# A fixed TensorE order, paired inversions and a spilled matrix in the scan of a hybrid RWKV-7 layer

## The chip, the cores and the metric

The kernel runs on one core of a Trainium2 chip. A core has five engines that run side by side: TensorE (matmuls, written PE in the profile, with its weight loads as PEld), VectorE (DVE), ScalarE (ACT), GpSimd (POOL) and SyncE (SP), which here only issues transfers. Each engine, and each queue of transfers, works through its instructions strictly in the order that was fixed when the program was compiled; semaphores make it wait for others. The metric is the device time of one execution in microseconds, as the median of several runs. Times of single instructions come from one profiled execution.

## What is computed

One layer of a latent generator: a modulated RMSNorm, one input projection (2048 to 6400 columns), a bidirectional RWKV-7 time mixing over 16 heads of 64, a pooling branch, and one output projection with a gated residual. There are 1024 latent tokens and 256 context tokens, whose final scan state is where the latent scans begin. Cut to what matters:

```python
def reference(x, c, ctx, ...):
    ...
    p_l = h_l @ w_in[l]
    p_c = h_c @ w_in[l]
    lat = rwkv_prepare(centred_token_shift(p_l[..., :N_SHIFT], shift_mu[l]), ...)
    cx = rwkv_prepare(centred_token_shift(p_c[..., :N_SHIFT], shift_mu[l]), ...)
    S0 = jnp.zeros((N_DIR, B, N_HEADS, HEAD_DIM, HEAD_DIM), jnp.float32)
    S_ctx, y_c = bidir_scan(S0, *cx)
    _, y_l = bidir_scan(S_ctx, *lat)
    ...
    out_l = branch_output(p_l, y_l, r_l, kd_l, v_l, ...)
    x = x + gt_l * out_l
    return rms_norm(x, final_g)

def _rwkv_step(S, inp):
    r, w, k, v, a, b = inp
    sa = jnp.einsum('dbhvk,dbhk->dbhv', S, a)
    S = S * w[..., None, :] + sa[..., :, None] * b[..., None, :] + v[..., :, None] * k[..., None, :]
    y = jnp.einsum('dbhvk,dbhk->dbhv', S, r)
    return S, y
```

## The kernel before

Three stages follow each other on the time axis.

**Preparation** (lines 185 to 546). Dense matmuls in three f16 products (`dense_mm`, lines 152 to 154) make the columns of r, k and v for the pairs of heads j = 0 to 7; `prep_scan` (line 422) turns them into the scan's operands and stores these in DRAM: `sAR` (A and R rows), `sBK` (B and K rows), `sV` and `sBV`. The work on pair j runs beside the dense matmuls of pair j + 1. Pair 7 has no successor: after its last dense tile only its own chain is left (the tail). Its last TensorE work is the bonus product (lines 497 and 498), in the PSUM banks B1 and A1.

**Scan** (lines 555 to 948). Time is cut into 20 chunks of 64 tokens, 4 context and 16 latent. Four quarters Q, each of four heads in both directions, go through 20 chunks, so there are 80 steps, in 20 batches of four. What a step needs:

- `scores` (line 650): 16 small f32 matmuls (as the profile counts them, two to a product) of the B/K rows with the A/R rows into the banks A0 and A1; VectorE masks them into NA and, for latent chunks, MR. Four diagonal blocks of NA go to a DRAM tile `dn`.
- `inverse` (line 688), once per batch: the 32 x 32 diagonal blocks of four steps are gathered from `dn` into TT, 64 on the partitions, and inverted on VectorE by 30 pairs of instructions (tm on line 702, TT on line 704). The result goes through DRAM into T, and TensorE joins the blocks with 64 + 64 tiny matmuls (lines 726 and 737).
- `step` (line 769): X = NA times SUV (line 787), a VectorE copy Xs, T times Xs (line 800), two VectorE copies into SUV, then the state product (line 811), the VectorE sum St, two VectorE products into the next step's SUV (line 818) and a GpSimd product S (line 819). The outputs of a latent step (lines 827 and 829, 32 matmuls) are emitted late, after X of the step behind it.
- `load_step` (line 743), one step ahead: v rows, A rows, B/K rows with four transposes (line 761), R.
- `finish` (line 854): normalisation and gating of two finished chunk pairs.

What is left of the dense input projection (24 tiles of 96 matmuls: gate and pooling columns) is the `filler`, a generator that is advanced one unit (12 dense matmuls) at a time by `pump`. One GpSimd queue (`idma`) and one SyncE queue (`dma`) carry the transfers.

The order on every engine, TensorE too, is made by the planner of the tile framework: it takes what is ready, by priority. A priority is the place in the program text, moved forward by the offset of a `high_priority` block: 800 for the four phases of a step, 1000 for the scores, inversions and finishes beside it, none for the filler. The first two batches are prepared ahead of the steps, with FILL0 = 10 units of filler in the text. Buffers: NA and MR ten each, TT two.

**Output projection** (lines 952 to 1044). 2 x 4 x 16 blocks of three fp32r products (line 981), residual and final norm.

Of the kernel before, what the change touches and what calls it, by code (L numbers as in the profile page):

```python
# [31 lines left out]
RING = 10  # L32
BVS = 2
WRAW = 2
FILL0 = 10
SCT = (1, 3, 5, 7)
INVT = 10
HP_STEP = 800
HP_SIDE = 1000
# [19 lines left out]
def hybrid_layer_kernel(ctx: ExitStack, tc: tile.TileContext, I, out, dbg=None):  # L59
# [22 lines left out]
    sV = dram.tile([4, NCH, 2, C, 2, C], F32, name="sV")  # L82
    sG = dram.tile([8, 128, NTOK], F32, name="sG")
# [471 lines left out]
    with ExitStack() as p2s:  # L555
# [31 lines left out]
        def pool_tile(jj, z):  # L587
            g = jj // 2
            win = WINDOWS[g]
            for x in lat_tile(34 + jj):  # L590
                if x is None:
                    yield
                    continue
                i, ps = x
                S.activation(up[:, :, 8:72], ps.rearrange("p (r t) -> p r t", t=C), AF.Copy, scale=1.0 / HW)
                a = p2.tile([128, 8, 80], F32, tag="pa", name=nm("pa"))
                V.tensor_tensor(a[:, :, 1:80], up[:, :, 0:79], up[:, :, 1:80], ALU.add)
                lo, hi, half = 1, 79, 1
                while 2 * half < win:
                    b = p2.tile([128, 8, 80], F32, tag="pb" if half != 2 else "pa", name=nm("pb"))  # L600
                    lo, hi = lo + half, hi - half
                    V.tensor_tensor(b[:, :, lo:hi + 1], a[:, :, lo - half:hi + 1 - half], a[:, :, lo + half:hi + 1 + half], ALU.add)
                    a, half = b, 2 * half
                zv = z[:, 512 * i:512 * i + 512].rearrange("p (r t) -> p r t", t=C)
                V.tensor_tensor(zv, a[:, :, 8:72], rc[:, g].unsqueeze(1).broadcast_to([128, 8, C]), ALU.mult)
                V.tensor_tensor(zv, zv, up[:, :, 8:72], ALU.subtract)
                yield

        def pool_group(g):
# [3 lines left out]
            for m in range(2):  # L613
                wpool = p2.tile([128, 2, 128], F32, tag="wpool", name=nm("wpool"))
                dma(wpool, I["w_pool"][:, g, :, 128 * m:128 * m + 128])
                for x in lat_tile(42 + 2 * g + m):
# [4 lines left out]
                    sg = silu_gate(ps)  # L621
                    for k in range(2):
# [16 lines left out]
        NFILL = 24 * 10  # L639

        st8 = {}

        hss = [slice(64 * h, 64 * h + 64) for h in range(2)]

        def get(Q, g):
            if (Q, g) not in st8:
                st8[(Q, g)] = dict(SUV=[], NA=[], MR=[], BKt=[])
            return st8[(Q, g)]

        def scores(Q, g, s):  # L650
            b = get(Q, g)
# [5 lines left out]
            dma(AR.rearrange("q a p d t -> q (a p d t)"), sAR[Q, c, :, 0:ns].rearrange("q a p d t -> q (a p d t)"))  # L657
            NA = p2.tile([128, 2, 2, 2, C], F32, tag="NA", bufs=RING, name=nm("NA"))
            MR = None
            if g:  # L660
                MR = p2.tile([128, 2, 2, 2, C], F32, tag="MR", bufs=RING, name=nm("MR"))
            b["NA"].append(NA)
            b["MR"].append(MR)
            ps = [bank(f"A{h}") for h in range(2)]
            for p in range(2):
                for d in range(2):
                    u = 2 * p + d
                    for h in range(2):
                        hs = hss[h]
                        mm(ps[h][:, 64 * ns * u:64 * ns * (u + 1)], BK[hs, p, d, :], AR[hs, :, p, d, :], start=True, stop=True)  # L670
            for h in range(2):
                pv = ps[h][:, 0:256 * ns].rearrange("q (p d a t) -> q p d a t", p=2, d=2, a=ns)
                V.tensor_tensor(NA[:, h], pv[:, :, :, 0, :],
                                mask[:, h, :, 0:64].unsqueeze(1).broadcast_to([128, 2, 2, C]), ALU.mult)
            if s == 0:
                b["dn"] = dram.tile([2, 2, 4, 4, 32, 32], F32, tag="dn", bufs=3, name=nm("dn"))
            for blk in range(2):
                for h in range(2):
                    rs = 64 * h + 32 * blk
                    dma(b["dn"][blk, h, s].rearrange("u s t -> s u t"),  # L680
                        NA[rs:rs + 32, h, :, :, 32 * blk:32 * blk + 32].rearrange("q p d t -> q (p d) t"))
            for h in range(2):
                if g:
                    pv = ps[h].rearrange("q (p d a t) -> q p d a t", p=2, d=2, a=2)
                    V.tensor_tensor(MR[:, h], pv[:, :, :, 1, :],
                                    mask[:, h, :, 64:128].unsqueeze(1).broadcast_to([128, 2, 2, C]), ALU.mult)

        def inverse(Q, g):
            b = get(Q, g)
            c0 = CCH * g  # L690
            NA = b["NA"]
            TTf = p2.tile([128, 32, 32], F32, tag="TT", bufs=2, name=nm("TT"))
            TT = TTf[0:64]
            idma(TT.rearrange("q a b -> q (a b)"), b["dn"].rearrange("k h c u s t -> (k h c u) (s t)"))
# [4 lines left out]
            for s in range(30, 0, -1):  # L699
                n = 31 - s  # L700
                tm = p2.tile([64, s, n], F32, tag="tm", name=nm("tm"))
                V.tensor_tensor(tm, TT[:, 0:s, s:s + 1].broadcast_to([64, s, n]),  # L702
                                TT[:, s:s + 1, s + 1:32].broadcast_to([64, s, n]), ALU.mult)
                V.tensor_tensor(TT[:, 0:s, s + 1:32], TT[:, 0:s, s + 1:32], tm, ALU.add)  # L704
                if s % 3 == 0:
                    yield
            V.memset(TT.rearrange("q a b -> q (a b)")[:, 0:1024:33], 1.0)
            T1c = TTf[64:96]
            V.tensor_copy(T1c, TT[0:32].rearrange("q a b -> q b a"))
            dt = dram.tile([2, 2, 16, 32, 32], F32, tag="dt", bufs=2, name=nm("dt"))  # L710
            dtt = dram.tile([2, 16, 32, 32], F32, tag="dtt", bufs=2, name=nm("dtt"))
            idma(dtt.rearrange("h u s t -> (h u) (s t)"), T1c.rearrange("q a b -> q (a b)"))
            idma(dt.rearrange("k h u s t -> (k h u) (s t)"), TT.rearrange("q a b -> q (a b)"))
            T1 = p2.tile([128, 16, 32], F32, tag="T1", name=nm("T1"))
            for h in range(2):
                idma(T1[64 * h:64 * h + 32], dtt[h].rearrange("u s t -> s u t"))
            for h in range(2):
                for blk in range(2):
                    rs = 64 * h + 32 * blk
                    idma(T[rs:rs + 32, :, 32 * blk:32 * blk + 32], dt[blk, h].rearrange("u s t -> s u t"))  # L720
# [22 lines left out]
        def load_step(Q, g, s):  # L743
            b = get(Q, g)
            SUV = p2.tile([128, 2, 2, 2, C], F32, tag="SUV", bufs=SVB, name=nm("SUV"))
            c = CCH * g + s
            for h in range(2):
# [3 lines left out]
            b["SUV"].append(SUV)  # L751
            for h in range(2):
                dma(b["NA"][s][hss[h], h].rearrange("q p d t -> q (p d) t"),
                    sAR[Q, c, hss[h], 0].rearrange("q p d t -> q (p d) t"))
            if c < NCH - 1:
                BK = p2.tile([128, 2, 2, 128], F32, tag="BK", bufs=BKB, name=nm("BK"))
                dma(BK.rearrange("q p d x -> q (p d x)"), sBK[Q, c].rearrange("q p d s t -> q (p d s t)"))
                BKt = p2.tile([128, 2, 2, 2, C], F32, tag="BKt", bufs=BTB, name=nm("BKt"))
                pst = bank(f"B{c % 2}")
                for u in range(4):  # L760
                    nc.tensor.transpose(pst[:, 128 * u:128 * u + 128], BK[:, u // 2, u % 2, :], ident)  # L761
                S.copy(BKt.rearrange("q p d h t -> q (p d h t)"), pst)
                b["BKt"].append(BKt)
            if g:
# [358 lines left out]
```

## Time and profile before

| | us |
|---|---|
| three runs, median (lowest to highest) | 2388.03 (2385.95 to 2404.02) |
| the profiled execution | 2389.13 |
| its span, first to last instruction | 2387.4 |
| last dense tile of pair 7 ends, first filler matmul | 897.0 |
| first scores matmul | 965.2 |
| first X | 1042.6 |
| last X | 1979.4 |
| last filler matmul | 2018.7 |

The mean granted clock was 0.988 of full speed. In a row of the stretches "busy" is the time in which at least one instruction of the engine was under way; matmuls are pipelined, so one starts before the one ahead has ended. A row of a group gives line, engine, operation, what is written and read, the shape and count, then busy us and mean ns, then the idle time ahead of it and what ended it. A row of the timeline gives start and length in us, and in square brackets the idle time ahead of it.

### The profile page before, as it was taken

How to read it: one execution, taken by the hardware profiler on the slowest of the kernel's cores; microseconds unless marked ns; L12 is line 12 of the kernel's file. 1: busy time of each engine (PE TensorE's matmuls, PEld its weight loads, DVE VectorE, ACT ScalarE, POOL GpSimd, SP SyncE). 2: the span in 40 equal slices, each digit the busy share in tenths (PEclk: the TensorE clock that was granted, in tenths of full speed). 3: DMA queues.
4: the chain of work that ended last, by engine and by line, in shares of the span. 5: the costliest groups of instructions: out<-in, count | busy, mean ns of one | idle time of the engine just before them, and what ended most of it. 6: DMA issues, size and time to landing. Idle time of an engine off the chain costs nothing. (4 is left out here: it accounts for less than half of the span.)

```text
span 2387.4 us, 50718 instructions
## 1 busy us (share of the span) xinstructions
PE 2252.8 (94%) x19854; PEld 1342.6 (56%) x19854; DVE 1637.4 (69%) x3432; ACT 785.7 (33%) x1307; POOL 380.2 (16%) x682
## 2 busy tenths in 40 slices
PE   2999999999999999899999999999999999999997
PEld 1445444454454454446655566556665655888886
DVE  7644756566466567588698888999888884345446
ACT  5334533444444434112122212312231222333424
POOL 3000000000000001023333333333333321000000
PEclk9999999999999999999899999999999999999999
DMA  8665556455354355655556556555666432645546
GB/s 309 218 215 159 152 144 157 134 147 147 96 129 113 87 138 144 175 152 145 159 147 169 151 141 181 165 148 158 179 171 167 134 95 92 234 133 169 190 128 207
DMA packets 421598, 374.60 MB, mean 157 GB/s; under 512 B 232984, under 2 KB 298552, under 8 KB 421104
## 3 DMA queue, kind: packets, MB, share of 16 engines
q1 hardware_dynamic: 403824, 331.75, 48.1%
q0 software_dynamic: 17536, 39.61, 5.8%
q8 instruction: 157, 2.57, 0.4%
q14 instruction: 81, 0.66, 0.1%
HBM read 286.53 MB, written 83.37 MB: 155 GB/s over the span
## 5 line engine op out<-in xcount | busy, mean ns | idle before, releaser
L152 PE MATMUL ps<-hhi,whi 128*128 128x512 f16 x1600 | 611.5, 383 | 2.6 <-ACT whi L144 2.0
L154 PE MATMUL ps<-hhi,wlo 128*128 128x512 f16 x1600 | 611.3, 383 | 1.4 <-DVE wlo L145 1.3
L153 PE MATMUL ps<-hlo,whi 128*128 128x512 f16 x1600 | 610.4, 382 | 0.4 <-DVE hlo L247 0.4
L152 PEld LDWEIGHTS <-whi 128*128 128x128 f16 x1888 | 185.2, 98 | 182.0 <-issue 27.6
L154 PEld LDWEIGHTS <-wlo 128*128 128x128 f16 x1888 | 185.0, 98 | 177.4 <-issue 18.1
L153 PEld LDWEIGHTS <-whi 128*128 128x128 f16 x1888 | 185.4, 98 | 165.7 <-issue 14.8
L144 ACT ACTIVATE whi<-wraw 128x512 f16<-128x512 f32 x200 | 123.1, 628 | 262.4 <-PE ps L153 196.3
L702 DVE TENSOR_TENSOR tm<-TT 64x30 f32<-64x30 f32 (+2 forms) x600 | 195.8, 326 | 16.8 <-DMA TT<-dn 7.9
L704 DVE TENSOR_TENSOR TT<-TT,tm 64x30 f32<-64x30 f32 (+2 forms) x600 | 196.5, 328 | 8.5
L981 PE MATMUL ps<-wolo,mhi 128*128 128x512 f32 x512 | 199.7, 390 | 2.2 <-DVE wolo L977 2.1
L977 DVE TENSOR_TENSOR wolo<-wo,wohi 128x512 fp32r<-128x512 f32 x144 | 97.9, 690 | 148.1 <-ACT wohi L976 147.9
L145 DVE SCALAR_TENSOR_TENSOR wlo<-wraw,whi 128x512 f16<-128x512 f32 x200 | 135.9, 684 | 92.2 <-ACT whi L144 90.8
L981 PE MATMUL ps<-wohi,mlo 128*128 128x512 f32 x512 | 198.9, 389 | 0.0
L981 PE MATMUL ps<-wohi,mhi 128*128 128x512 f32 x512 | 198.2, 390 | 0.4 <-ACT wohi L976 0.4
L976 ACT CAST wohi<-wo 128x512 fp32r<-128x512 f32 x144 | 89.1, 621 | 177.3 <-PE ps L981 150.1
L670 PE MATMUL ps<-AR,BK 64*128 64x128 f32 (+1 forms) x1280 | 121.7, 294 | 16.3 <-DMA BK<-sBK 7.3
L670 PEld LDWEIGHTS ps<-AR,BK 64*128 64x128 f32 x1280 | 104.5, 196 | 44.7 <-issue 14.6
L750 POOL DMA_DIRECT2D SUV<-sV x160 | 96.6, 607 | 124.9 <-PE ps L811 62.4
L981 PEld LDWEIGHTS ps<-wolo,mhi 128*128 128x128 f32 x512 | 96.1, 188 | 24.1 <-DVE wolo L977 4.2
L981 PEld LDWEIGHTS ps<-wohi,mhi 128*128 128x128 f32 x512 | 95.9, 188 | 21.6 <-ACT wohi L976 2.0
L981 PEld LDWEIGHTS ps<-wohi,mlo 128*128 128x128 f32 x512 | 96.1, 188 | 19.7
L819 POOL TENSOR_TENSOR S<-St,PCt 128x256 f32<-128x256 f32 x76 | 56.9, 749 | 258.1 <-DVE St L813 228.6
(226 smaller groups left out, 3379.3 us busy)
## 6 DMA issues: line engine op xcount, KB each, us to landing
wraw<-in_w_in SPq DMA_DIRECT2D x200, 256.0 KB, 3.4
BK<-sBK SPq DMA_DIRECT2D x156, 256.0 KB, 3.5
wo<-in_w_out SPq DMA_DIRECT2D x144, 256.0 KB, 3.0
wa<-in_w_ada SPq DMA_DIRECT2D x112, 256.0 KB, 3.1
wg<-in_w_ada SPq DMA_DIRECT2D x64, 256.0 KB, 3.1
AR<-sAR SPq DMA_DIRECT2D x64, 256.0 KB, 3.0
sBK<-BK SPq DMA_DIRECT2D x32, 320.0 KB, 3.9
sBK<-BK SPq DMA_DIRECT2D x16, 640.0 KB, 5.5
```

The lines of the kernel that those rows point to most:

```text
L144: S.activation(whi, raw, AF.Copy, scale=WS)
L145: V.scalar_tensor_tensor(wlo, raw, WS, whi, op0=ALU.mult, op1=ALU.subtract)
L152: mm(ps[:, :n], w[0][:, k, :], hi[kt][:, o:o + n], start=(kt == 0), stop=False)
L153: mm(ps[:, :n], w[0][:, k, :], lo[kt][:, o:o + n], start=False, stop=False)
L154: mm(ps[:, :n], w[1][:, k, :], hi[kt][:, o:o + n], start=False, stop=(kt == KT - 1))
L670: mm(ps[h][:, 64 * ns * u:64 * ns * (u + 1)], BK[hs, p, d, :], AR[hs, :, p, d, :], start=True, stop=True)
L702: V.tensor_tensor(tm, TT[:, 0:s, s:s + 1].broadcast_to([64, s, n]), TT[:, s:s + 1, s + 1:32].broadcast_to([64, s, n]), ALU.mult)
L704: V.tensor_tensor(TT[:, 0:s, s + 1:32], TT[:, 0:s, s + 1:32], tm, ALU.add)
L750: (idma if d else dma)(SUV[hss[1 - h], h, :, d, :], sV[Q, cn, h])
L976: S.copy(whi, raw)
L977: V.tensor_tensor(wlo, raw, whi.bitcast(F32), ALU.subtract)
L981: mm(banks[q, t], mix[k][m][:, tk], w, start=(k == order[0] and n == 0), stop=(k == order[-1] and n == 2))
```

## The change

TensorE's order in the scan is no longer planned. The whole scan stands in a block in which TensorE keeps the order of the text; the other engines are still planned, with new offsets (steps 800, side work 600, inversions 100). The text is written out step by step in `run_step`: X, the outputs of the step before, T, scores of the step 15 ahead (LEAD), state product, transposes of the next step, then filler in three portions, 2.15 units a step while there are scores and 3.2 in the last 15. Ahead of the steps stand 15 times one unit and one `scores`, then the first assembly with four units.

Two batches are inverted at once: `inverse(i)` works on 128 partitions for the batches 2i and 2i + 1, in the second to sixth of eight steps, and the joining of the blocks moves into `assemble`, once per batch (in the seventh and eighth step for the first batch of the pair, in the following first and second for the other). NA has 15 buffers. MR has two; it is stored to a DRAM tile `sMR` after its scores and loaded again one step before its outputs. Loads are split off: `score_loads` one step ahead of the scores, `step_loads` and the A rows (`a_rows`) one step ahead of X. The sums of the pooling branch go in two halves, and the pool product has a unit of its own.

```diff
-RING = 10
+RING = 15
...
-FILL0 = 10
-SCT = (1, 3, 5, 7)
-INVT = 10
+LEAD = 15
+FILLS = (2.15, 3.2)
 HP_STEP = 800
-HP_SIDE = 1000
+HP_SIDE = 600
+HP_INV = 100
...
+    sMR = dram.tile([4, NCH - CCH, 128, 512], F32, name="sMR")
...
+                for q in range(2):
+                    r4 = slice(4 * q, 4 * q + 4)
+                    a = p2.tile([128, 4, 80], F32, tag="pa", name=nm("pa"))
+                    V.tensor_tensor(a[:, :, 1:80], up[:, r4, 0:79], up[:, r4, 1:80], ALU.add)
...
                     sg = silu_gate(ps)
+                    yield
...
+            if g:
+                MR = p2.tile([128, 2, 2, 2, C], F32, tag="MR", bufs=2, name=nm("MR"))
+                for h in range(2):
+                    V.tensor_tensor(MR[:, h], pv[h][:, :, :, 1, :],
                                     mask[:, h, :, 64:128].unsqueeze(1).broadcast_to([128, 2, 2, C]), ALU.mult)
-
-        def inverse(Q, g):
+                dma(sMR[Q, c - CCH], MR.rearrange("q h p d t -> q (h p d t)"))
+
+        def inverse(i):
+            TT = p2.tile([128, 32, 32], F32, tag="TT", name=nm("TT"))
+            idma(TT.rearrange("q a b -> q (a b)"), dns[i].rearrange("k e h c u s t -> (k e h c u) (s t)"))
+            for s in range(30, 0, -1):
+                n = 31 - s
+                tm = p2.tile([128, s, n], F32, tag="tm", name=nm("tm"))
...
+        def run_step(k):
+            r = k % 8
+            part = FILLS[k + LEAD >= NST] / 3
+            inv = invs.get(k // 8 + 1)
+            last = k == NST - 1
+            with chain():
+                phase_x(k)
+            with side():
+                if not last:
+                    step_loads(k + 1)
+                    if (k + 1) % 4:
+                        a_rows(k + 1)
+                if k + LEAD + 1 < NST:
+                    score_loads(k + LEAD + 1)
+                if r in (0, 6) and k // 4 + 1 + (r == 6) * 0 < len(batches):
+                    asm["now"] = assemble(k // 4 + 1)
+                    next(asm["now"])
+                if st.get("late"):
+                    outputs()
+                elif k:
+                    suv.pop(k - 1)
+            if not (k and steps[k - 1][1]):
+                pump(1)
+                owed[0] -= 1
+            with chain():
+                phase_t(k)
+            with side():
+                if r in (1, 7) and "now" in asm:
+                    run(asm.pop("now"))
+                    if r == 7 and not last:
+                        a_rows(k + 1)
+                if k + LEAD < NST:
+                    scores(k + LEAD)
+                else:
+                    fin_tick()
+            with chain():
+                phase_s(k)
+            with side():
+                if r == 3 and not last:
+                    a_rows(k + 1)
+                if not last:
+                    turned(k + 1)
+            pump(part)
+            with tc.high_priority(offset=HP_INV):
+                if r == 0 and k // 8 + 1 < NST // 8:
+                    invs[k // 8 + 1] = inverse(k // 8 + 1)
+                elif inv is not None and 1 <= r <= 5:
+                    for _ in range(2 + (r == 5)):
+                        next(inv, None)
+            pump(part)
+            with side():
+                if r in (0, 6) and "now" in asm:
+                    next(asm["now"])
+                fin_tick()
+            pump(part)
+            with side():
+                fin_tick()
+
+        with tc.manual_schedule(engines={mybir.EngineType.PE}):
+            for k in range(LEAD):
+                with side():
+                    score_loads(k)
+                pump(1)
+                with side():
+                    scores(k)
+                    if k == 7:
+                        invs[0] = inverse(0)
+                    elif k > 7:
+                        next(invs[0], None)
+                        next(invs[0], None)
+            with side():
+                score_loads(LEAD)
+                run(invs[0])
+                step_loads(0)
+                asm["now"] = assemble(0)
+                next(asm["now"])
+            pump(1)
+            with side():
+                turned(0)
+            pump(1)
+            with side():
+                next(asm["now"])
+            pump(1)
+            with side():
+                run(asm.pop("now"))
+                a_rows(0)
+            pump(1)
+            for k in range(NST):
+                run_step(k)
+            with side():
+                if st.get("late"):
+                    outputs()
+            run(fill)
+            for f in fins:
+                run(f)
```

More of the change, by code (lines that the diff above doesn't have):

```diff
@@ L750, in load_step @@
                     (idma if d else dma)(SUV[hss[1 - h], h, :, d, :], sV[Q, cn, h])
-            b["SUV"].append(SUV)
-            for h in range(2):
[L753 to L763, printed above, removed]
@@ new lines, in turned, with phase_x @@
+        def turned(k):
+            if k not in ins:
+                return
+            BK = ins.pop(k)
+            BKt = bkts[k] = p2.tile([128, 2, 2, 2, C], F32, tag="BKt", bufs=BTB, name=nm("BKt"))
+            pst = bank(f"B{k % 2}")
+            for u in range(4):
+                nc.tensor.transpose(pst[:, 128 * u:128 * u + 128], BK[:, u // 2, u % 2, :], ident)
+            S.copy(BKt.rearrange("q p d h t -> q (p d h t)"), pst)
+        st = {}
+        def phase_x(k):
+            Q, g, s = steps[k]
+            NA, SUV = get(Q, g)["NA"].pop(s), suv[k]
+            if g + s == 0:
+                S0 = st["S"] = p2.tile([128, 4, C], F32, tag="S", bufs=2, name=nm("S"))
@@ L790, in step @@
[L790 to L800 removed]
+            XU = st["XU"] = bank("XU")
+            for u in range(4):
+                for h in range(2):
+                    mm(XU[hss[h], 64 * u:64 * u + 64], NA[:, h, u // 2, u % 2, :], SUV[:, h, u // 2, u % 2, :],
+                       start=True, stop=True)
@@ L801, in step, with phase_t @@
+            Xs = st["Xs"] = p2.tile([128, 4, C], F32, tag="Xs", name=nm("Xs"))
+            V.tensor_copy(Xs.rearrange("q u v -> q (u v)"), XU[:, 0:256])
+        def phase_t(k):
+            Q, g, s = steps[k]
+            T, XU, Xs, SUV = get(Q, g)["T"], st["XU"], st["Xs"], suv[k]
+            for u in range(4):
+                for h in range(2):
+                    mm(XU[hss[h], 256 + 64 * u:320 + 64 * u], T[hss[h], 4 * s + u, :], Xs[hss[h], u, :], start=True, stop=True)
             for h in range(2):
@@ L847, in step, with outputs @@
-            if g:
-                if last:
-                    outputs()
-                else:
-                    carry["late"] = outputs
-            yield
+                st["S"] = Sn
+            st["late"] = (k, DY, S0) if g else None
+        def outputs():
+            k, DY, S0 = st["late"]
+            Q, g, s = steps[k]
+            SUV, MR, R = suv.pop(k), mrs.pop(k), rts.pop(k)
+            ous = [(u, h, DY[hss[h], 256 + 64 * u:320 + 64 * u]) for u in range(4) for h in range(2)]
+            for u, h, o in ous:
+                mm(o, MR[:, h, u // 2, u % 2, :], SUV[:, h, u // 2, u % 2, :], start=(u == 0), stop=False)
+            for u, h, o in ous:
+                mm(o, R[hss[h], u // 2, u % 2, :], S0[hss[h], u, :], start=False, stop=(u == 3))
+            i = CCH * g + s - CCH
+            if i == 0:
+                st["y"] = {}
+            ys = st["y"]
+            if i < 8 and i % 2 == 0:
+                m = (6 - i) // 2
+                ys[m] = p2.tile([128, 2, 2, 2, C], F32, tag=f"y{m}", name=nm("y"))
+            yv = DY[:, 256:512].rearrange("q (p d v) -> q p d v", p=2, d=2)
+            for d in range(2):
+                cn = 15 - i if d else i
+                m = (7 - cn) // 2 if cn < 8 else (cn - 8) // 2
+                y = ys[m][:, :, cn // 8, cn % 2, :]
+                if i < 8:
+                    S.copy(y, yv[:, :, d, :])
+                else:
+                    V.tensor_tensor(y, yv[:, :, d, :], y, ALU.add)
+            if i > 8 and i % 2:
+                fins.append(finish(Q, (i - 9) // 2, ys[(i - 9) // 2]))
```

262 lines of the change are left out of this document (95 added, 167 removed).

## The prediction

> **What bounds the kernel now.** I read the page first, then the busy time by stretch, then the timeline around one step, then the counts by line. The columns of the stretches are: length, busy us (x instructions) of PE, PEld, DVE, ACT, POOL, then granted clock, DMA share, GB/s.
>
> ```profile
> span 2387.4 us, 50718 instructions
> PE 2252.8 (94%) x19854; PEld 1342.6 (56%) x19854; DVE 1637.4 (69%) x3432; ACT 785.7 (33%) x1307; POOL 380.2 (16%) x682
> ```
> ```profile
> 897.00:956.00 59.00, 57.62 (x267) 26.00 (x266) 44.68 (x55) 25.87 (x36) 9.91 (x20) 1.00 0.57 151
> 956.00:1042.00 86.00, 76.80 (x492) 39.60 (x491) 56.47 (x152) 11.24 (x19) 9.52 (x15) 0.94 0.58 164
> 1042.00:1979.00 937.00, 906.09 (x11836) 565.52 (x11834) 798.20 (x2209) 217.62 (x401) 316.00 (x496) 0.99 0.55 153
> 1979.00:2021.00 42.00, 41.67 (x283) 20.33 (x283) 13.65 (x27) 8.64 (x15) 3.13 (x5) 1.00 0.24 79
> ```
>
> TensorE is the bound everywhere the change reaches. The stretches are: the tail of the preparation (to 956), scores and first inverse (to 1042), the 80 steps (to 1979), filler left over (to 2021). In the last three TensorE idles 9.2 + 30.9 + 0.3 = 40 us, and the clock (0.94 of 86 us, 0.99 of 937 us) costs 5 + 9 = 14 us more: some 55 us are there to be won as waits. VectorE is the second engine, 798 of 937 us.
>
> Busy time hides a second loss, which the timeline of one step shows in its start times.
>
> ```profile
> 1503.38 0.38 PE L154 MATMUL ps<-hhi,wlo 128*128 128x512 f16 x1
> ...
> 1503.69 0.68 PE L800 MATMUL ps<-Xs,T 64*64 64x64 f32 x16
> ...
> 1504.30 0.39 PE L152 MATMUL ps<-hhi,whi 128*128 128x512 f16 x1
> ...
> 1505.17 0.38 PE L153 MATMUL ps<-hlo,whi 128*128 128x512 f16 x1
> ...
> 1505.48 0.33 PE L811 MATMUL ps<-SUV,BKt 128*64 128x64 f32 x2
> ...
> 1505.74 0.39 PE L154 MATMUL ps<-hhi,wlo 128*128 128x512 f16 x1
> ...
> 1505.97 0.38 PE L152 MATMUL ps<-hhi,whi 128*128 128x512 f16 x1
> ...
> 1506.28 0.68 PE L811 MATMUL ps<-SUV,BKt 128*64 128x64 f32 x14
> ...
> 1506.89 0.39 PE L153 MATMUL ps<-hlo,whi 128*128 128x512 f16 x1
> ...
> 1509.07 0.68 PE L787 MATMUL ps<-SUV,NA 128*64 128x64 f32 x14 [0.16 <-DVE SUV L818]
> ...
> 1509.68 0.56 PE L829 MATMUL ps<-S,R 64*64 64x64 f32 x12
> ```
>
> A dense matmul lasts 0.38 us but, dense after dense, the next starts 0.216 us later; before a small f32 one it takes 0.31 (1503.38 to 1503.69, 1505.17 to 1505.48), so going into small work costs 0.09. Small matmuls start about 0.04 apart, and the last of a block needs some 0.15 to the next dense one (14 of L811 take 0.61: 13 x 0.035 + 0.15), so going back costs 0.11. One excursion is 0.2 us, all of it "busy". A change between two kinds of small work costs about 0.1 (14 of L787 take 0.61 to L829). TensorE leaves the dense stream 418 times between 950 and 2025 in the timeline, one step's S product even in two pieces as above: 418 x 0.2 = 84 us, and about 350 changes among the small kinds, 35 us.
>
> The Trainium skill, "Trainium Kernel Development and Optimization", section Performance Expectations, calls matmul busy time a bad metric of how near a kernel is to its bound, because matmuls are pipelined. The trace agrees (0.38 long, 0.216 apart). By busy time alone the order of the instructions could win nothing beyond the idle 40 us, and the sum below would be 2452 in place of 2404.
>
> **The change part by part.**
>
> *1. The cover of the preparation's tail goes: +49 us.* Columns as above, of one line alone; then rows of TensorE, SyncE's queue and ScalarE.
>
> ```profile
> 897.00:956.00 59.00, 30.59 (x81) 7.85 (x81) 1.00 0.57 151
> ...
> 897.00:956.00 59.00, 30.20 (x81) 7.93 (x81) 1.00 0.57 151
> ...
> 897.00:956.00 59.00, 29.96 (x79) 7.77 (x80) 1.00 0.57 151
> ```
> ```profile
> 951.15 0.81 PE L497 MATMUL ps<-kdh,headr 128*128 128x512 f32 x2
> ...
> 965.23 1.11 PE L670 MATMUL ps<-AR,BK 64*128 64x64 f32 x16 [1.77 <-DMA AR<-sAR]
> ```
> ```profile
> 954.20 0.33 SPq L500 DMA_DIRECT2D sBV<-bv  x1
> ...
> 956.97 0.86 SPq L766 DMA_DIRECT2D R<-sAR  x2
> ...
> 959.94 0.42 SPq L656 DMA_DIRECT2D BK<-sBK  x1
> ```
>
> From 897 the last head pair's preparation is a chain of VectorE and DMA work. TensorE stays busy only because the scheduler pulls 81 + 81 + 79 = 241 dense filler matmuls (20 units of 12) ahead of the first scores. In the new text the order on TensorE is one unit, scores(0), one unit, scores(1). scores(0) takes bank A1, which the last bonus product (L497 at 951, i = 1) holds, and its loads stand on SyncE's queue behind the last store of the preparation (954.20). So scores(0) comes at about 957 at best (issue plus some 3 us), and only one unit, 12 matmuls, can stand before it. The other 229 are paid later: 229 x 0.216 = 49 us. The tail itself I take as no shorter: its chain runs through VectorE and stores, not through the filler.
>
> *2. Fewer changes of kind: -48 us.* In the new text a step is X, outputs, T, scores, S, turn, then about 2.15 units in one piece. Dense blocks: 80 (steps) + 17 (the unit after X where there are no outputs) + 14 and 8 (third unit behind an assemble or a finish) + 19 (lead) + 32 (pool products) = 170, at 0.2 = 34 us. Changes among small kinds: some 0.45 us a step, 36 us. Before 84 + 35 = 119, after 70. The work itself (dense, scores, X, T, S, outputs, turns, assembles) is the same number of instructions.
>
> *3. Two batches in one inversion: VectorE -206 us, on the path nothing by itself.*
>
> ```profile
> L704 DVE TENSOR_TENSOR TT<-TT,tm 64x30 f32<-64x30 f32 (+2 forms) x600 | 196.5, 328 | 8.5
> L702 DVE TENSOR_TENSOR tm<-TT 64x30 f32<-64x30 f32 (+2 forms) x600 | 195.8, 326 | 16.8 <-DMA TT<-dn 7.9
> ...
> L802 DVE COPY SUV<-ps 64x256 f32<-64x256 f32 x160 | 67.1, 419 | 22.5 <-PE ps L800 19.2 <-issue 0.4
> ...
> L789 DVE COPY Xs<-ps 128x256 f32<-128x256 f32 x80 | 32.8, 410 | 7.1 <-PE ps L787 6.2 <-PE ps L827 0.9
> ```
>
> A copy on 128 partitions takes what one on 64 takes (410 against 419 ns), so 1200 instructions become 600 at the same 0.33: -196 us, and ten transposed copies of 1.03 fewer, -10. VectorE falls from 798 to about 600 of some 940 us. The halved pool sums add a few us there, hidden. VectorE is not the bound, so this pays only through shorter waits (part 5). The price is the delay of the first inversion (part 5).
>
> *4. MR through DRAM, loads a step ahead: 0.* Per step one store and one load of 256 KB more; on SyncE's queue two issues of about 0.4 (rows like the BK load above), 8 to 9 us of a step of 11.7 (937 / 80). The DMA engines stand at 0.55. MR's load waits for the outputs of the step before and holds behind it on SyncE the A rows and the score loads of the next step; they have a step in hand. If that cover went, each late load would stop TensorE, 0 to 1 us a step; nearest row 0.86 for two issues. I take 0.
>
> *5. Waits: 55 before, 69 after: +14 us.*
>
> ```profile
> 1511.71 1.05 DVE L709 COPY TT<-TT 32x1024 f32<-32x1024 f32 x1
> ...
> 1512.91 0.40 DVE L789 COPY Xs<-ps 128x256 f32<-128x256 f32 x1
> ...
> 1513.37 0.54 PEld L800 LDWEIGHTS ps<-Xs,T 64*64 64x64 f32 x16 [0.60 <-DVE Xs L789]
> ```
> ```profile
> 1027.26 1.08 POOL L713 DMA_DIRECT2D dt<-TT  x1 [10.87 <-DVE tm L702]
> ...
> 1032.29 1.29 POOL L716 DMA_DIRECT2D T<-dtt  x2
> ```
> ```profile
> L726 PE MATMUL ps<-T,NA x1280: 184/191/254, 1037.7 to 1946.4; 32*32 32x32 f32 x183
> ```
>
> X was done at 1509.75 (L787 above), its copy ran at 1512.91: VectorE's queue delays a hand-off by 3 us today and TensorE fills the time with whatever is ready. With a fixed order the cover is what the text puts there. X to T: copy 0.41 and about 0.2 of signalling against 32 output matmuls, 1.24 us; T to S: two copies, 0.84 + 0.2, against 16 score matmuls, 1.3 us. The cover is enough unless VectorE is inside another instruction (0.3 to 1.05 us). I take 0.2 a step over 65 steps, 13 us; bounds 0 and 1.0. In the last 15 steps there are no scores behind T: 1.1 each, 16 us. First inversion: it needs eight steps' scores and shares VectorE with seven more; from its last instruction to L726 the trace has 10.4 us (1027.3 to 1037.7), while TensorE's lead text holds about 72 us of work: a wait of 15 us, bounds 0 and 30. Nine later assembles, 1 us each, bounds 0 and 5. The last finish is no longer covered by dense work after 1979: 6 us. Clock: 10. Sum 69.
>
> *Sum:* 49 - 48 + 14 = +15. The profiled execution took 2389.1 us (span 2387.4 and 1.7 around it), 1.1 above the median 2388.0 of the three runs. 2389.1 + 15 = 2404 us.
>
> **The rivals.**
>
> *A, faster: the scores start inside the tail.* If the planner puts scores(0) and the next ones ahead of the bonus product, the 15 units of the lead, 180 matmuls, fill the tail and part 1 falls to about zero: 2404 - 49 = 2355. For it: the loads now carry a priority. Against it: bank A1, and the first instruction of the scan's pool runs at 948 today, behind the last head pair's sum:
>
> ```profile
> 948.36 0.31 POOL L777 MEMSET S<- 128x256 f32 x1 [1.36 <-DVE kds L487]
> ```
>
> *B, slower: the hand-offs decide.* Each step has two places (T and S) where TensorE now stands still if VectorE is late. The wait of 3.2 us above, of which the cover takes 1.2, is what such a place can cost. With 0.8 us a step in place of 0.2, 80 x 0.6 = 48: 2452. From 0.3 us a step on (0.2 + 8/80) the result is over 1% slower. For it: VectorE carries in five of eight steps all inversions, about 3.9 us on top of 6. Against it: it has 200 us less to do.
>
> *C, slower: each inversion ends late and stops TensorE.* The two-batch inversion ends in the sixth of eight steps, its assemble stands at the end of the seventh, 10 us later, about what store and load take. If it is 4 us late each time, 9 x 4 = 36: 2440.
>
> ```profile
> 965.00:990.00 25.00, 23.95 (x149) 12.83 (x150) 8.04 (x16) 1.82 (x3) 0.54 (x1) 0.86 0.47 132
> ...
> 1165.00:1190.00 25.00, 24.87 (x307) 16.79 (x308) 15.80 (x46) 3.65 (x9) 6.00 (x10) 0.88 0.46 128
> ```
> The granted clock has dips of 0.86 and 0.88 over 25 us, 3 us each; the first follows the idle 1.77 before L670 at 965, so gaps of 4 us could cost 3 more each: 9 x 3 = 27, 2467 with C. The Trainium skill, "TensorE: Matmul & The Clock Gate", in the table under "Why this matters for your kernels", warns of idle gaps over about 3 us, after which the clock halves; the dips agree in kind, though gaps of under 3 us stand before them here.
>
> **How the numbers follow.** Forecast (waits as summed, part 1 in full): 0.42, own range 2380 to 2425. A 0.22. B 0.24. C 0.12. About 1%, 24 us, is what a measurement of this kernel can tell from no change, so under 2364 is faster and over 2412 slower. The forecast holds the middle, A the faster side, B and C the slower: 0.22, 0.42, 0.36. The range for 8 in 10 reaches from just under A's 2355 to B's 2452, 2350 to 2452.
>
> **What would show it.** Part 1: dense filler matmuls before 956 fall from 241 to about 12, and TensorE is idle for some 45 us before the first scores. If it is busy there, A holds. Part 2: a timeline with dense runs of 12 to 36 and some 170 excursions. Part 3: tm and TT rows x300 each at 0.33. Part 5: TensorE's idle in the steps, by what ended it: Xs and SUV copies (B), T loads or the assemble (C). I am wrong if the idle time in the tail stays small, or if the steps hold under 15 or over 100 us of waits.

## The result and the profile after

| | before | after |
|---|---|---|
| median, us (lowest to highest) | 2394.07 (2385.95 to 2404.02) | 2422.64 (2419.09 to 2425.25) |
| the profiled execution, us (span) | 2389.13 (2387.4) | 2419.09 (2417.3) |
| first filler matmul, first scores, first X | 897.0, 965.2, 1042.6 | 894.0, 954.1, 1046.2 |
| dense filler matmuls ahead of the first scores | 274 | 12 |
| last X, last filler matmul | 1979.4, 2018.7 | 2029.4, 2042.6 |

The changed kernel takes 1.0116 times as long, 95% interval 1.0068 to 1.0165: 28 us or 1.2% slower, in four runs of each. The prediction had 2404 us; its sum was +15 us on the profiled execution, which became +30.

The page of the kernel after, then its four stretches (columns as in the prediction: length, busy us and instructions of PE, PEld, DVE, ACT, POOL, granted clock, DMA share, GB/s):

```profile
span 2417.3 us, 50344 instructions
PE 2169.6 (90%) x19854; PEld 1312.0 (54%) x19854; DVE 1495.2 (62%) x2868; ACT 794.4 (33%) x1311; POOL 356.4 (15%) x652
```
```profile
894.00:954.00 60.00, 11.84 (x38) 4.27 (x36) 37.67 (x43) 19.00 (x24) 5.89 (x15) 0.57 0.45 111
954.00:1046.00 92.00, 75.65 (x588) 40.54 (x588) 44.47 (x124) 7.96 (x14) 16.04 (x25) 0.85 0.73 211
1046.00:2029.00 983.00, 892.78 (x12070) 565.89 (x12072) 681.21 (x1692) 241.56 (x429) 290.66 (x464) 0.97 0.61 178
2029.00:2050.00 21.00, 17.03 (x181) 9.28 (x180) 9.13 (x19) 6.01 (x11) 2.58 (x4) 1.00 0.39 127
sum 1156.00, PE 997.30 PEld 619.97 DVE 772.48 ACT 274.52 POOL 315.17; mean PE 249.32 PEld 154.99 DVE 193.12 ACT 68.63 POOL 78.79
```

These rows hold the whole account. Before, the same work filled 1124 us (897 to 2021) with 1082 us of busy TensorE; now it fills 1156 with 997. TensorE issues the same 19854 matmuls and is busy 85 us less, which is what the order was to bring and more. But it stands idle for 159 us in place of 42: 117 us of new waits. Together that is 32 us more; the stretch begins 3 us earlier than before and 1 us more follows it, so 30 remain. What TensorE waited for from 890 to 2060 (waiting instruction, what ended the wait, us in total, times, longest):

```profile
PE ps L826 <- DVE Xs L819: 38.4, 26, 3.8
PE ps L498 <- ACT kdh L492: 37.4, 1, 37.4
PE ps L628 <- DVE sg L576: 21.5, 10, 3.7
PE ps L839 <- DVE SUV L828: 20.2, 20, 4.5
PE ps L153 <- ACT whi L145: 10.4, 1, 10.4
PE ps L839 <- DVE y L875: 8.0, 6, 2.6
PE ps L682 <- DMA AR<-sAR: 7.0, 2, 5.8
```

Second row: the preparation's tail, where the bonus product (L498) now waits in the open. L826 is T times Xs and L839 the state product, the two hand-offs of a step: 38.4 + 20.2 + 8.0 = 66.6 us (in the last of the three, the instruction of VectorE that came last is not the copy SUV but the sum y of the outputs). L628 is the product of the pooling branch, which the prediction did not have. The assembles (L749, L760) stand under other rows with 0.9 us in all.

Two hand-offs that are late. First the longest wait for Xs, in the timeline around step 26:

```profile
1351.16 0.69 PE L816 MATMUL ps<-SUV,NA 128*64 128x64 f32 x16
...
1352.24 0.68 PE L859 MATMUL ps<-S,R 64*64 64x64 f32 x16
...
1352.90 0.68 DVE L146 SCALAR_TENSOR_TENSOR wlo<-wraw,whi 128x512 f16<-128x512 f32 x1
...
1355.40 0.36 DVE L712 TENSOR_TENSOR TT<-TT,tm 128x198 f32<-128x198 f32 x1
...
1356.28 0.42 DVE L819 COPY Xs<-ps 128x256 f32<-128x256 f32 x1
...
1356.75 1.12 PE L826 MATMUL ps<-Xs,T 64*64 64x64 f32 x16 [3.83 <-DVE Xs L819]
```

X is done at 1351.85. VectorE does not wait here: it works through ten instructions of the inversion and two that make filler weights (wlo), which stand ahead of the copy Xs in its order, for 4.4 us. The outputs of the step before end at 1352.92, and TensorE waits 3.83 us. Then another kind, around step 41:

```profile
1541.09 0.69 PE L816 MATMUL ps<-SUV,NA 128*64 128x64 f32 x16
...
1544.10 0.38 PE L155 MATMUL ps<-hhi,wlo 128*128 128x512 f16 x1
...
1544.58 0.20 DVE L710 TENSOR_TENSOR tm<-TT 128x30 f32<-128x30 f32 x1 [6.48 <-DMA TT<-dn]
...
1547.28 0.42 DVE L819 COPY Xs<-ps 128x256 f32<-128x256 f32 x1
...
1547.76 1.12 PE L826 MATMUL ps<-Xs,T 64*64 64x64 f32 x16 [3.28 <-DVE Xs L819]
```

X is done at 1541.78, and VectorE is free. But the first instruction of the next inversion stands ahead of the copy Xs in VectorE's fixed order, and waits 6.48 us for the load of TT. Then ten instructions of the inversion run, and only then Xs. The twelve dense matmuls behind X end at 1544.5, and TensorE waits 3.28 us. VectorE is not short of time here (4.00 us busy of the 8 from 1541); it waits for the wrong thing.

The first kind costs more. Of the 67 us, counted wait by wait in the timeline, 25 are waits for Xs in 15 steps in which VectorE ran the inversion between X and the copy, on average five of its instructions. A load of TT for which VectorE stood still accounts for 16 us, in seven waits at both hand-offs. The state product of the last 15 steps, which have no scores in front of it, waits 12 us; the rest is 14 us. By line, in the 80 steps (busy us, mean ns, idle time ahead):

```profile
L710 DVE TENSOR_TENSOR tm<-TT 128x30 f32<-128x30 f32 (+5 forms) x270 | 88.9, 329 | 43.6 <-DMA TT<-dn 37.3
L712 DVE TENSOR_TENSOR TT<-TT,tm 128x30 f32<-128x30 f32 (+5 forms) x270 | 88.8, 329 | 6.5
```

### The profile page after: what moved, and what is told of

Same layout as the page of the kernel before. It is cut to its first block, busy times and chain, and to the rows that moved or that the text cites. A ratio compares the mean times of both kernels' runs of the same rounds, so it can differ in the third digit from the quotient of the medians.

```text
span 2417.3 us, 50344 instructions
## 1 busy us (share of the span) xinstructions
PE 2169.6 (90%) x19854; PEld 1312.0 (54%) x19854; DVE 1495.2 (62%) x2868; ACT 794.4 (33%) x1311; POOL 356.4 (15%) x652
## 5 line engine op out<-in xcount | busy, mean ns | idle before, releaser
L153 PE MATMUL ps<-hhi,whi 128*128 128x512 f16 x1600 | 614.0, 384 | 11.0 <-ACT whi L145 10.4
L801 ACT COPY BKt<-ps 128x512 f32<-128x512 f32 x76 | 44.5, 586 | 276.0 <-PE ps L800 275.8
L710 DVE TENSOR_TENSOR tm<-TT 128x30 f32<-128x30 f32 (+5 forms) x300 | 98.8, 329 | 50.6 <-DMA TT<-dn 43.6
L682 PE MATMUL ps<-AR,BK 64*128 64x128 f32 (+1 forms) x1280 | 98.6, 295 | 10.7 <-DMA AR<-sAR 7.0
L712 DVE TENSOR_TENSOR TT<-TT,tm 128x30 f32<-128x30 f32 (+5 forms) x300 | 98.7, 329 | 7.3
L682 PEld LDWEIGHTS ps<-AR,BK 64*128 64x128 f32 x1280 | 83.6, 198 | 22.2 <-issue 10.2
```

What stands on the lines that cost most here:

```text
L153: mm(ps[:, :n], w[0][:, k, :], hi[kt][:, o:o + n], start=(kt == 0), stop=False)
L682: mm(ps[h][:, 64 * ns * u:64 * ns * (u + 1)], BK[hs, u // 2, u % 2, :], AR[hs, :, u // 2, u % 2, :], start=True, stop=True)
L710: V.tensor_tensor(tm, TT[:, 0:s, s:s + 1].broadcast_to([128, s, n]), TT[:, s:s + 1, s + 1:32].broadcast_to([128, s, n]), ALU.mult)
```

## The experiments

Before's median moved between 2388.6 and 2394.9 us from one set of runs to another, so differences between kernels are taken from their ratios to before, times 2390. The ratio of the kernel after is known to 0.005, 12 us. "Steps" is the time from the first X to the last (after: 983 us; before: 937).

**The tail's cover.** Fifteen units of filler go ahead of the lead; the steps get fewer.

```diff
-FILLS = (2.15, 3.2)
+FILLS = (1.95, 3.05)
+            pump(15)
             for k in range(LEAD):
```

> 15 filler units are put in the text ahead of the first scores, and taken from the steps (FILLS 1.95 and 3.05). If the lost cover of the preparation's tail is the main loss, TensorE's idle time of 51 us between 900 and 954 falls to about 8, 180 dense matmuls (39 us) leave the steps, and the time falls by about 39 us to 2384 (before: 2394). Rival, waits in the steps decide and less filler there only makes them longer: the tail is filled but the steps give most of it back, 2405 or more.

Measured: 2388.86 us, ratio 1.0011 (0.9987 to 1.0035), 25 us less than after. TensorE's idle time in the tail falls from 48 to 17 us, and from the first filler matmul (896.8) to the first scores (965.4) it is 69 us again, where after has 60.

```profile
897.00:965.00 68.00, 51.19 (x216) 21.96 (x214) 44.98 (x55) 25.53 (x36) 11.02 (x22) 0.87 0.55 146
965.00:1055.00 90.00, 73.25 (x588) 39.43 (x588) 52.18 (x142) 9.38 (x16) 11.20 (x18) 0.89 0.72 207
1055.00:2000.00 945.00, 853.90 (x11906) 547.41 (x11906) 664.72 (x1663) 232.17 (x416) 289.00 (x465) 0.97 0.62 183
```

So the lost cover is a real term. The filler does lengthen the tail, by 8 to 9 us, which the prediction had ruled out. And 180 dense matmuls taken out of the steps, 39 us at 0.216, shorten these by 38 (983 to 945).

**The inversion's place on VectorE.** First only in the text: TT is loaded in the first step of eight, and its instructions stand in the third to sixth.

```diff
+            yield
             for s in range(30, 0, -1):
...
-                elif inv is not None and 1 <= r <= 5:
-                    for _ in range(2 + (r == 5)):
+                elif inv is not None and 2 <= r <= 5:
+                    for _ in range(3):
```

> The load of TT is asked for in the first of eight steps, as now, but the first VectorE instruction of the inversion comes in the third step, not in the second; it ends in the sixth as before. If T waits because the inversion's instructions stand ahead of the Xs copy on VectorE and wait there for TT to land (43.6 us of VectorE's idle time, T's 34 us of waits in the first 65 steps), VectorE's wait for TT falls under 10 us, T's waits under 18, and the time by 15 to 20 us to about 2404. Rival, T waits because VectorE has too much work in these steps: four steps now hold what five held, T's waits stay or grow, 2420 to 2430.

Measured: 2415.05 us, 1.0129 (1.0080 to 1.0179). The edit did not reach its aim: VectorE's order is still planned, tm still stands ahead of Xs (waits for TT 47.0 us, T times Xs 37.4). It tells nothing about the theory. So a small copy was added, which makes the first tm depend on the Xs of the third step:

```diff
+                if s == 30 and i:
+                    V.tensor_copy(tm[:, 0, 0:1], st["Xs"][:, 0, 0:1])
```

> The first VectorE instruction of an inversion now also waits for the Xs copy of the third of eight steps (a copy of one column), so the planner can't put the inversion ahead of the hand-offs of the second and third step. If T waits because the inversion stands ahead of Xs on VectorE, waiting there for TT (47 us of VectorE's idle time), that idle time falls under 5 us, T's waits in the second and third steps fall from 24 to under 8, and the time falls by about 15 us from the changed kernel's 2422 to 2407. Rival, VectorE simply has too much to do in these steps: T's waits move to the fourth to sixth steps and the time stays at 2415 to 2430.

Measured: 2449.57 us, 1.0242 (1.0208 to 1.0276), 30 us more than after.

```profile
PE ps L752 <- DMA T<-dtt: 37.9, 13, 8.4
...
PE ps L829 <- DVE Xs L822: 29.7, 25, 5.8
```

The edit reaches its aim: VectorE's wait for TT falls from 43.6 to 6.1 us. The hand-off waits fall with it, from 66.6 to 49.4 us, but that for Xs only by 9. So the load that stands ahead of the copy is worth about 17 of the 67 us; the inversion's instructions, which still run ahead of later copies, are left. And the assembles (L752) now wait 37.9 us for T, where after has 0.9. The inversions begin 0.8 of a step later than in the kernel after and end 1.2 steps later, and the prediction's rival C appears: they have no slack. The early place that makes Xs late is also what keeps the assembles on time.

**The pool product's wait.** The product is held back behind the next dense unit (its tile gets a second buffer).

```diff
-FILLS = (2.15, 3.2)
+FILLS = (1.98, 2.95)
...
+                if pend:
+                    pend.pop()()
...
-                    yield
-                    for k in range(2):
-                        mm(ps, wpool[:, k, :], ...)
+                    def product(i=i, ps=ps, sg=sg, wpool=wpool, m=m):
+                        for k in range(2):
+                            mm(ps, wpool[:, k, :], ...)
...
+                    pend.append(product)
```

> The pool product is moved behind the next dense unit in place of a unit of its own. If its 21.5 us of waits for the gate's SiLU come only from standing directly behind it in the text, they fall to about 1 and the time by 15 to 21 us to about 2404. Rival, TensorE reaches a later wait sooner and stands there instead: the line's wait goes but the time falls by under 5.

Measured: 2389.05 us, 0.9988 (0.9962 to 1.0015), 31 us less than after, with the tail left open. Steps 947 us. The wait for sg falls from 21.5 to 4.8 us, and that for Xs from 38.4 to 21.4, more than the wait itself:

```profile
PE ps L835 <- DVE Xs L828: 21.4, 22, 2.8
...
PE ps L633 <- DVE sg L580: 4.8, 4, 1.7
```

In a fixed order a late product holds back everything written behind it; that this is how the hand-offs gain too is a reading, which no run shows by itself.

**The fixed order itself.** The block that fixes TensorE's order is replaced by an empty one; all else stays.

```diff
-        with tc.manual_schedule(engines={mybir.EngineType.PE}):
+        with ExitStack():
```

> All of the change but the fixed order: the planner orders TensorE again. If the fixed order itself costs the time (the tail and the waits of T, S and the pool product), the tail is filled again, excursions rise from 129 to some 400, TensorE's idle time falls from 156 to about 45, and the time goes back to about 2390, perhaps 10 less for the paired inversion. Rival, the paired inversion, MR through DRAM or the loads cost it: it stays at 2410 or more.

Measured: 2593.48 us, 1.0870 (1.0819 to 1.0921). The planner fills the tail again (260 dense matmuls before the first scores), and TensorE idles only 87 us. But it leaves the dense stream 408 times, changes 1026 times among small kinds (after: 485), and its granted clock in the steps is 0.89; they take 1043 us with 511 dense matmuls still to come after them. With this text and these offsets the fixed order is not the loss: planned, they are far worse. The offsets of the kernel before were not tried with the rest of the change.

**VectorE's relief.** The paired inversion is kept, but each instruction is split into two halves of 64 partitions, 1200 in place of 600.

```diff
-                V.tensor_tensor(tm, ...)
-                V.tensor_tensor(TT[:, 0:s, s + 1:32], ...)
+                for e in range(2):
+                    hs = slice(64 * e, 64 * e + 64)
+                    V.tensor_tensor(tm[hs], ...)
+                    V.tensor_tensor(TT[hs, 0:s, s + 1:32], ...)
```

> The inversion's instructions are issued for each half of the 128 partitions by itself, 1200 of 0.33 us in place of 600, so VectorE has some 196 us more to do in the same order of steps. If VectorE's free time is worth nothing, as the prediction had it, the time stays within 5 us of 2422. Rival, VectorE's length sets the hand-offs: T's and S's waits grow by 20 us or more and so does the time.

Measured: 2655.32 us, 1.1119 (1.1091 to 1.1147), 240 us more than after, though VectorE is busy only 862 us of 1202 in the steps:

```profile
PE ps L751 <- DMA T<-dtt: 115.8, 15, 16.6
PE ps L828 <- DVE Xs L821: 76.5, 36, 5.9
...
1070.00:2272.00 1202.00, 952.49 (x12090) 599.93 (x12090) 862.21 (x2230) 239.63 (x426) 289.13 (x466) 0.89 0.50 145
```

VectorE is busy 181 us more in the steps, and the kernel takes 240 us more. In this order the inversion's work on VectorE is on the path. The edit makes each inversion longer and VectorE busier at once, so it does not tell these two apart. Waits for T are the largest part, 115.8 of TensorE's 250 idle us in the steps; its busy time grows by 60 us too, at a granted clock of 0.89.

**MR's way through DRAM.** First twice over: a second store and load of the same data, read by nobody.

```diff
+                dma(sMR2[Q, c - CCH], MR.rearrange("q h p d t -> q (h p d t)"))
...
+                MX = p2.tile([128, 512], F32, tag="MX", bufs=2, name=nm("MX"))
+                dma(MX, sMR2[Q, c - CCH])
```

> Each MR is stored twice, to two DRAM tiles, and each is loaded (the second copy isn't read): two more issues on SyncE's queue a latent step, about 0.8 us, and 33 MB more traffic. If MR's way through DRAM is hidden, as the prediction had it, the time stays within 5 us of 2422. Rival, SyncE's queue or the DMA engines set the pace of the steps: 64 x 0.8 = 51 us more, 2470.

Measured: 2470.16 us, 1.0341 (1.0310 to 1.0373), 54 us more than after. Then not at all; the outputs multiply with the mask in MR's place, so this kernel leaves out part of the computation and serves for its time alone:

```diff
-                dma(sMR[Q, c - CCH], MR.rearrange("q h p d t -> q (h p d t)"))
...
-                dma(MR.rearrange("q h p d t -> q (h p d t)"), sMR[Q, c - CCH])
...
-                mm(o, MR[:, h, u // 2, u % 2, :], SUV...)
+                mm(o, mask[:, h, u % 2, 64:128], SUV...)
```

> The changed kernel with MR's way through DRAM left out: VectorE still makes MR, but it is neither stored nor loaded, and the outputs multiply with the mask in its place. 64 stores and 64 loads of 256 KB go, and with them two of some nine issues a step on SyncE's queue and the wait of MR's load for the outputs of the step before. The prediction's theory (MR through DRAM costs nothing on the path): 2417 to 2427, as the changed kernel. The rival, from the run in which MR was stored and loaded twice (+48 us): 30 to 48 us less, 2375 to 2390; the waits of SyncE's queue for the outputs (62.9 us, 21 times) go, the DMA share in the steps falls from 0.62 to about 0.55, and TensorE's waits for T and SUV fall from 68 us to under 45. A time between 2390 and 2417 would say that the first trip costs less than a second one does.

Measured: 2403.84 us, 1.0035 (1.0015 to 1.0055), 19 us less than after (with its uncertainty of 12): between the theories, so the first trip costs less than a second one, and not nothing. Steps 966 us. SyncE's queue, its largest wait in total from 890 to 2060, after and then without the trip:

```profile
SPq L784 <- PE ps L857: 77.0, 23, 12.2
```
```profile
SPq L775 <- PE ps L854: 87.1, 30, 10.2
```

Here the expectation was wrong: the wait for the outputs does not go with MR's load (L784), for the load of R (L775), which stands next, takes it over. TensorE's hand-off waits shrink only from 66.6 to 57.1 us (30.2 + 19.0 + 7.9), and the one wait of 10.4 for whi disappears, while one of 9.7 for T takes its place ahead of the steps, so that from the first scores to the first X both kernels take 92 us and the gain lies in the steps.

Two waits follow the number of trips (none, one, two): VectorE's for TT with 33.8, 43.6 and 51.2 us, and TensorE's for the filler's weights (whi) with 0, 10.4 and 27.6. After the first scores, the first load of filler weights leaves SyncE's queue at 982.8 us without the trip, at 1007.0 with one and at 1021.0 with two.

**Combinations.** The cover and the later product together, with FILLS = (1.78, 2.75):

> Both the 15 filler units ahead of the first scores and the pool product behind the next dense unit. Each alone gave some 33 us. If they are separate losses (the tail's cover; waits in the steps with the half-rate clock behind them), the gains add up to about 60 and the time is about 2358, faster than before by 1.3%. Rival, TensorE's next limit is near: under 2375 isn't reached.

Measured: 2387.86 us, 0.9993 (0.9967 to 1.0019). The two gains, 25 and 31 us, do not add; the sum is 29. Steps 941 us, hand-off waits 69 us, assembles 9.7. Then the held inversion on top, and a dense unit between T and S in the last 15 steps:

> As the kernel before it in this list, with the inversion held behind Xs as well, and in the last 15 steps one filler unit between T and S. If hand-offs without cover are the loss there (11 us of S waits in the last 15 steps, 20 of T), the late S waits fall under 2 us and the time by another 10 to 25, to about 2340. Rival, the unit between T and S only moves the wait to X or delays the chain: within 5 us of the kernel without it.

Measured: 2415.93 us, 1.0108 (1.0072 to 1.0144). The waits for SUV shrink from 28.9 to 3.9 us, but the assembles wait 64.3 us: again the inversion has no time to give. What is left is to start it earlier. LEAD and RING become 16, and the load of TT and the inversion move ahead by one step (eighth of the previous eight, first to sixth):

```diff
-RING = 15
+RING = 16
-LEAD = 15
+LEAD = 16
...
-                if r == 0 and k // 8 + 1 < NST // 8:
-                    invs[k // 8 + 1] = inverse(k // 8 + 1)
-                elif inv is not None and 1 <= r <= 5:
-                    for _ in range(2 + (r == 5)):
+                if r == 7 and k // 8 + 2 < NST // 8:
+                    invs[k // 8 + 2] = inverse(k // 8 + 2)
+                    next(invs[k // 8 + 2])
+                elif inv is not None and r <= 5:
+                    for _ in range(2):
```

> Scores run 16 steps ahead (NA has 16 buffers), so each inversion may begin one step earlier, with six steps in place of five. If the inversion's place in the eight steps is the tight one (T waits behind it at its front, and the joining of the blocks waits for it when it ends later), T's waits of 38 us fall under 25, the half-rate time of 92 us falls with them, and the time goes to about 2400. Rival, the planner puts the inversion's instructions ahead of the hand-offs wherever it begins: T's waits stay at 30 to 40 and the time at 2415 to 2425.

Measured: 2417.43 us, 1.0102 (1.0078 to 1.0126): alone no difference to after that can be measured, though the wait for Xs falls from 38.4 to 28.5 us and the steps take 972 in place of 983. With the cover and the later product:

> The kernel with 15 units in front and the pool product later (2388) with 16 steps of lead. Its steps took 941 us with 1848 dense matmuls, as long as others with 2040, so something other than TensorE's work sets their length. If that is the inversion's cycle of eight steps, a step more for it shortens them: about 920 us, 2365 in all. Rival, it is the chain of hand-offs X, T, S on VectorE itself: 935 to 945 us, 2385.

Measured: 2364.28 us, 0.9886 (0.9867 to 0.9906), 55 us less than after and 1.1% faster than the kernel before.

```profile
1062.00:1983.00 921.00, 848.59 (x11902) 548.41 (x11904) 664.31 (x1659) 225.08 (x409) 289.17 (x464) 0.97 0.63 186
```

The steps take 921 us, 20 less than in the combination without the earlier inversion. The assembles wait 2.0 us in place of 9.7, and the state product waits 17.9 us for SUV in place of 28.9. Here the two gains nearly add: 52 of 25 + 31.

## Why the prediction was right, and where it was not

The time fell on the predicted side of before and within the range, but its two halves were both too small. In the prediction's sum TensorE's busy time fell by 52 us (48 for the changes of kind, 4 of the clock) and its idle time rose by about 67 (49 in the tail, 18 of waits). Measured: -85 and +117. Each half was off by more (33 and 50 us) than the sum (15); that they have opposite signs, and the time so near, is luck.

*Part 1, the cover (+49).* Right in kind: 12 dense matmuls before the first scores, TensorE busy 11.8 us of the first 60, L498 waiting 37.4. Rival A is out. The step "the tail itself I take as no shorter" failed: it is 60 us in place of 68, and the cover run confirms that filler there lengthens it by as much. Against that, the filler lost was counted only to 956: 274 - 12 = 262 matmuls are 57 us. 57 - 8 = 49, so the size came out by two errors that cancel. Giving back 180 of the 262 (39 - 9 = 30 us by this count) gained 25.

*Part 2, fewer changes of kind (-48).* Right in kind, too small. Counted in the timeline from the first filler matmul to the output projection, TensorE leaves the dense stream 129 times (425 before), where 170 were predicted: 296 at 0.2 are 59 us. Changes among small kinds went from 622 to 485, where the prediction had 350 and 360: 137 at 0.1 are 14 more. That gives 73 of the 85 us.

*Part 3, the paired inversion (0 on the path).* The instructions are as predicted (300 of each at 0.33), but VectorE's busy time in the steps falls only from 798 to 681 us, where about 600 were forecast. "On the path nothing by itself" does not hold in the fixed order: in the run with halves 181 us more of it cost 240. The prediction priced it against the kernel before, where TensorE could take other work.

*Part 4, MR through DRAM (0).* Mis-sized. Without the trip the kernel is 19 us faster, with a second one 54 slower. The cover that was named (a step in hand for what is queued behind the load) is not enough. The likely way to TensorE is SyncE's queue, where other loads and stores stand behind MR's: the waits for TT and for the filler's weights grow with each trip. The transfers themselves and another planned order on the queue are not ruled out, with a DMA share of 0.53, 0.61 and 0.68 in the steps of the three kernels; no run separates these. The queue's wait for the outputs does not depend on MR's load.

*Part 5, waits.* The places were right, the sizes not. Hand-offs: 13 + 16 = 29 predicted, 66.6 measured. The step that failed is "the cover is enough unless VectorE is inside another instruction": not one instruction of up to 1.05 us stands ahead of a late copy but several, in the 15 steps above five of the inversion on average and up to ten (timeline around step 26). Some 16 us come from an instruction that waits for a transfer in VectorE's order (timeline around step 41). The last 15 steps were near the forecast, 12 us for 16. The steps hold 90 us of waits in all, under the 100 at which the prediction called itself wrong. Rival B had the place and 48 us as its price; 38 more than forecast came, but the larger gain of part 2 paid for most of it. The pool product's 21.5 us were not seen at all: the unit of its own was in the change's description, and an activation on ScalarE between a unit and its product is a third hand-off. The first inversion (15) and the assembles (9) cost about nothing: rival C did not come, though the held inversion shows how near it was.

*The clock (10).* After, it is short of full by 0.15 of 92 us and 0.03 of 983: 43 us, before by 5 + 9 = 14. Much of this lies in the waits themselves, so its price is anything up to the 29 us between them; no run here separates it. It is already inside the busy and idle times above.

That the gains of single repairs do not add at LEAD 15 and do at LEAD 16 fits an inversion whose cycle of eight steps has just enough time: what shortens a step without starting the inversion earlier brings the wait for T forward. The held inversion, the halves and the combination all point there. It is not shown by a run in which nothing but the inversion's length changes.

## What to carry to other kernels

When an engine's order is fixed by hand, price each hand-off by what stands ahead of the answering instruction in the other engine's queue, loads that are waited for there included, and not by that engine's busy share. A planner that fills gaps hides costs (a long inversion, a late product, an open tail), and all of them come due on the day its freedom is taken; look for every place where the new text puts a producer and its consumer next to each other. Repairs can wait for one another: the later product and the cover gave 29 us together, and 52 once the inversion began earlier, which alone gave nothing that could be measured.

## What the hardware showed that was not expected

The granted clock fell to 0.50 while TensorE was busy without a gap. In the run with the planned order, three stretches of 5 us, first the work of all engines (columns as above), then the matmuls of one dense line alone (busy us of PE and PEld, granted clock, DMA share, GB/s); the two other dense lines are as empty:

```profile
1255.00:1260.00 5.00, 5.00 (x51) 3.73 (x52) 0.48 (x2) 0.45 (x1) 0.00 (x0) 0.50 0.24 69
1260.00:1265.00 5.00, 5.00 (x34) 2.81 (x28) 1.38 (x2) 1.60 (x4) 2.74 (x4) 0.50 0.48 139
1265.00:1270.00 5.00, 5.00 (x32) 3.85 (x30) 1.63 (x4) 2.40 (x3) 0.31 (x1) 0.50 0.31 97
```
```profile
1255.00:1260.00 5.00, 0.00 (x0) 0.00 (x0) 0.50 0.24 69
1260.00:1265.00 5.00, 0.00 (x0) 0.00 (x0) 0.50 0.48 139
1265.00:1270.00 5.00, 0.00 (x0) 0.00 (x0) 0.50 0.31 97
```

For 15 us TensorE ran f32 matmuls only, nearly all of them small, and no dense f16 one, at half the clock; 14 of T times Xs take 1.11 us there. The Trainium skill, "TensorE: Matmul & The Clock Gate", Part 1, lets the clock fall after an idle window and rise after some 3.4 us of sustained work. Here it stayed low through work without a gap, so what counts as busy there is not what the trace counts: in this stretch, keeping small f32 matmuls on TensorE did not keep its clock up. Nor do they hold it down: from 1272.5 to 1274.5, still ahead of the next dense matmul (1274.61), the granted clock is 1.00, and 16 of T times Xs take 0.68 us. What decides between the two no run shows.
